# Gated factors of w_down loaded from ScalarE's queue, a new order of the seven products, and last weights split a step later

## The chip, the cores and the metric

The kernel runs on one core of a Trainium2 chip. The metric is the device time of one execution in microseconds, as the median of several runs. The names of the engines are those of the profile: PE (TensorE, the matmuls), DVE (VectorE), ACT (ScalarE), POOL (GpSimd) and SP (SyncE, which only starts transfers). Before the change the transfers spoken of here are started by SP and by POOL; the profile lists them as SPq and POOLq.

## The reference, cut to what matters

A block of an encoder works on 512 tokens of width 2048: RMSNorm, an input projection, an mLSTM with 4 heads beside a differential attention with 8, an output projection with residual, and then the channel mixer, in which the change lies. All inputs are float32.

```python
D_MODEL = 2048; D_FF = 5632
h2 = rmsnorm(x, norm2_g[l])
x = x + (jax.nn.silu(h2 @ w_gate[l]) * (h2 @ w_up[l])) @ w_down[l]
return rmsnorm(x, final_g)
```

## The kernel before, in words

**Numbers in two parts.** Matmuls take a rounded 32-bit type. So each factor is split: ACT writes the rounded part (`hi`, the cast of L98) and DVE the remainder (`lo`, L99), and three matmuls hi*hi, hi*lo and lo*hi make one product in PSUM. A split needs ACT, then DVE, for every tile that PE is to read.

**The down stage.** 16 of the 22 blocks of 256 rows of `w_down` go through a fast scheme that multiplies 2x2 blocks with seven products, P1 to P7, in place of eight. The 16 blocks make 4 chunks (`NSP`), and each chunk is done for two halves of the columns: 8 steps, which the text numbers `u` = 0 to 7, with chunk `ci = u // 2` and half `dg = u % 2`. A step goes through the seven names in the order of the list `DOWN`. Each product is 24 matmuls of 128x512, in two halves `h` of the contraction, 12 matmuls for each. In the first chunk ACT copies the products to the tiles `M` (L1088), afterwards DVE adds to them there (L1090).

**Its weights.** `left_factors` is a generator that yields one split weight factor for each half of a product; `factor` keeps it two factors, so one product, ahead of PE (`LAP`), and the tiles `whi` and `wlo` are rings of three. Per step it needs, for each half, the blocks B11, B22 and B21 as they are, and T1 and T3, sums of two blocks each: a plain load by SP (L889) with a second, accumulating load by POOL behind it (L891). These 512 KB loads fill the rings `raw` (first halves) and `raw2` (second halves), seven tiles each. P1 uses B11, P3 uses B22, P2 uses B21, P5 uses T1 and P7 uses T3. P6 uses B22 + T1, which DVE writes over B22 (L913), and P4 adds B21 to that (L915), again over B22. `upto` sets how far ahead loads are put into the program.

**Its gated factors.** The gate and up stage stores silu(gate)*up in DRAM, as the seven combinations that the scheme needs (`actv`). `variant` brings back the two 128x512 halves of one of them, 256 KB each (L956), and splits them to `A` tiles; they are what PE holds against the weight factors. The tile is `ra`, a ring of two, or `raw` for the first four names, which `group` asks for during its last call. Three more names come during step 0. Those of a next chunk come during the odd steps, one name per product. SP starts all of these loads.

**What sets the order of the work.** The code is written in one stream, and a scheduler places the instructions of each engine by priority, so the order on an engine is not always that of the code. An engine runs its own instructions in order: a DMA issue that waits for a buffer holds what stands behind it on that engine. In the built program, transfers started by SP and by ACT take turns on eight completion counters; a start waits until the transfer before it on its counter has landed.

**The tail.** After the down stage, `combine` adds the M tiles up, `proj_tok` does four more blocks of `w_down`, and the last two blocks and the final norm end the kernel. `last_weights` loads the weights of these last two blocks (L1171) and splits them, a piece at each call from `at`.

Of the kernel before, what the change touches and what calls it, by code (L numbers as in the profile page):

```python
# [19 lines left out]
NSP = 4  # L20
# [10 lines left out]
def build(nc, tc, ctx, a, out):  # L31
# [49 lines left out]
    V, SC, G, PE = nc.vector, nc.scalar, nc.gpsimd, nc.tensor  # L81
# [7 lines left out]
    c = {}  # L89
# [6 lines left out]
    def split(hi, lo, src, scale=None):  # L96
        if scale is None:
            SC.copy(hi, src)  # L98
            V.tensor_tensor(lo, src, hi.bitcast(F32), ALU.subtract)  # L99
        else:  # L100
            SC.activation(hi, src, AF.Copy, scale=scale)
            V.scalar_tensor_tensor(lo, src, scale, hi.bitcast(F32), ALU.mult, ALU.subtract)
# [734 lines left out]
    actv = dram.tile([4 * NSP, 7, 128, 256], F32, name="actv")  # L837
# [4 lines left out]
    def tW(tag, dt=F32, bufs=3):  # L842
        return pW.tile([128, 1024], dt, tag=tag, name=nm(tag), bufs=bufs)

    DOWN = ["P1", "P3", "P6", "P5", "P7", "P4", "P2"]
    more = []

    def tR():
# [2 lines left out]
    def left_factors():  # L851
        def loads(w, g):
            r = []
            for q in range(4):
                t = tW("raw", bufs=7)
                nc.sync.dma_start(t, a[w][g, q])
                r.append(t)
            return r

        def parts(src):  # L860
            hi, lo = tW("whi", F32R), tW("wlo", F32R)
            split(hi, lo, src)
            return hi, lo

        todo = [(w, g) for g in range(NFB) for w in ("w_g", "w_u")]
        nxt = loads(*todo[0])
        for i in range(len(todo)):
            w11, w12, w21, w22 = nxt
            yield parts(w11)
            s1 = tW("raw", bufs=7)  # L870
            V.tensor_tensor(s1, w21, w22, ALU.add)
            V.tensor_tensor(w21, w11, w21, ALU.subtract)
            V.tensor_tensor(w11, s1, w11, ALU.subtract)
            yield parts(w11)
            yield parts(w21)
            yield parts(s1)
            if i + 1 < len(todo):
                nxt = loads(*todo[i + 1])
            yield parts(w12)
            yield parts(w22)  # L880
            V.tensor_tensor(w12, w12, w11, ALU.subtract)
            yield parts(w12)


        def load(u, h, i, ring):
            j, n, j2, n2 = ((0, 0, 0, 0), (1, 1, 1, 1), (0, 0, 0, 1), (1, 1, 0, 1), (1, 0, 1, 0))[i]
            ci, dg = divmod(u, 2)
            t = ring()
            nc.sync.dma_start(t, a["w_ds"][ci, dg, j, n, h])  # L889
            if (j, n) != (j2, n2):  # L890
                G.dma_start(t, a["w_ds"][ci, dg, j2, n2, h], accum_op=ALU.add)  # L891
            return t

        order = [(u, i, h) for u in range(2 * NSP) for i in range(5) for h in range(2)]
        got = {}
        pos = [0]

        def upto(k):
            while pos[0] < min(k, len(order)):
                u, i, h = order[pos[0]]  # L900
                got[u, i, h] = load(u, h, i, tR if h and (u, i) != (0, 0) else lambda: tW("raw", bufs=7))
                pos[0] += 1

        upto(2)
        for u in range(2 * NSP):
            k = 10 * u
            for pi, name in enumerate(DOWN):
                if u or pi:
                    upto(k + (14 if pi == 0 else 16 if pi < 6 else 20))
                for h in range(2):  # L910
                    B11, B22, T1, T3, B21 = (got.get((u, i, h)) for i in range(5))
                    if name == "P6":
                        V.tensor_tensor(B22, B22, T1, ALU.add)  # L913
                    if name == "P4":
                        V.tensor_tensor(B22, B22, B21, ALU.add)  # L915
                    yield parts({"P1": B11, "P3": B22, "P6": B22, "P5": T1, "P7": T3, "P4": B22, "P2": B21}[name])
# [26 lines left out]

    cur_v = {}

    def variant(ci, name, into):

        v = ["P1", "P7", "P2", "P4", "P5", "P6", "P3"].index(name)
        into[name] = []
        for h in range(2):  # L950
            if more:
                r = more[2].tile([128, 512], F32, tag="ra", name=nm("ra"), bufs=2)
            else:
                r = tW("raw", bufs=7)[:, 0:512]
            g0 = 4 * ci + 2 * h
            nc.sync.dma_start(r.rearrange("p (g c) -> p g c", g=2), actv[g0:g0 + 2, v].rearrange("g p c -> p g c"))  # L956
            hi, lo = tA(), tA()
            split(hi, lo, r)
            into[name].append((hi, lo))

    def group(scale, done, first=False, last=False):

        banks = {}
        ps, u, C1, C2 = (tX() for _ in range(4))
# [45 lines left out]
        for name in order:  # L1010
            w = factor()
            product(bank(name), w, name_of(name))
            if first and name == "P2":
                next(st2)
            after(name)
            if last:
                i = {"P1": 0, "P6": 1, "P5": 2, "P4": 3}.get(name)
                if i is not None:
                    variant(0, DOWN[i], cur_v)

    def name_of(p):
        return RIGHT[p]
# [46 lines left out]
    for u in range(2 * NSP):  # L1069
        ci, dg = divmod(u, 2)  # L1070
        got_v = cur_v
        if dg == 1:
            cur_v = {}
        for pi, name in enumerate(DOWN):
            if u == 0 and pi < 3:
                variant(0, DOWN[4 + pi], cur_v)
            if dg == 1 and ci + 1 < NSP:
                variant(ci + 1, name, cur_v)
            banks = [tacc(), taux()]
            for h in range(2):  # L1080
                product_down(banks, factor(), name, h)
            if ci == 0:
                M[dg][name] = pM.tile([128, 1024], F32, tag="M", name=nm("M"), bufs=14)
            t = M[dg][name]
            for tt in range(2):
                cs = slice(tt * 512, tt * 512 + 512)
                if ci == 0:
                    SC.copy(t[:, cs], banks[tt])  # L1088
                else:
                    V.tensor_tensor(t[:, cs], banks[tt], t[:, cs], ALU.add)  # L1090
# [75 lines left out]
    def last_weights():  # L1166

        for b in range(CHUNKS[-1]):
            for n in range(4):
                r = tW("raw", bufs=7)  # L1170
                nc.sync.dma_start(r, a["w_d"][NFB - CHUNKS[-1] + b, n])  # L1171
                for j in range(2):
                    hi, lo = tL(), tL()
                    split(hi, lo, r[:, j * 512:j * 512 + 512])
                    wL[n][0].append(hi)
                    wL[n][1].append(lo)
                yield

    for ci, nb in enumerate(CHUNKS[:-1]):
        q = chunks[ci]  # L1180
# [31 lines left out]
    for tt in range(4):  # L1212
# [14 lines left out]
        r = tsm(1, tag="rf")  # L1227
# [99 lines left out]
```

## Time and profile before

| | |
|---|---|
| median of 3 runs | 2180.97 us |
| lowest and highest run | 2178.7 and 2186.47 us |
| the profiled execution's own time | 2190.05 us |
| span of the profiled execution | 2188.3 us |
| granted clock of PE, mean over the span | 0.991 |
| PE, DVE, ACT, POOL busy | 98%, 72%, 45%, 6% of the span |
| the down stage | 1691.3 to 2044.4 us of the span |

The span runs from the first to the last instruction that the profiler saw; the execution's own time has 1.75 us more around it. A busy share is one over stages with different limits, so the rows further down cut the down stage into its steps. A granted clock of 1.00 is 2.4 GHz, and the lower level is 1.2 GHz.

### The profile page before, as it was taken

Reading aid. Unit: us, or ns where it says so; the run is one execution under the profiler, and the core shown is the slowest. Engines: PE = TensorE matmul, PEld = TensorE weight load, DVE = VectorE, ACT = ScalarE, POOL = GpSimd, SP = SyncE. Lnnn points to the kernel's source line nnn. Section 1 sums busy time; section 2 is a strip of 40 time slices with the busy share of each in tenths; the row PEclk is TensorE's granted clock in tenths of the full one; section 3 lists DMA queues with packets and bytes.
Section 4 is the critical chain, followed back from the end, with each engine's and each line's share of the span. In section 5 each row is a group of like instructions: output and inputs, shape, how many; then the busy total and the mean of one; then the engine's idle time right before and its main releaser. Section 6 shows DMA issues by size and latency. Waiting matters only on the chain.

```text
span 2188.3 us, 33437 instructions
## 1 busy us (share of the span) xinstructions
PE 2142.0 (98%) x13305; PEld 1938.2 (89%) x13305; DVE 1569.6 (72%) x2362; ACT 992.7 (45%) x1515; POOL 133.8 (6%) x189
## 2 busy tenths in 40 slices
PE   9999999999999999999999999999999799999998
PEld 7888889988888889999999999999999577778786
DVE  6267776366544468888888888888889467779745
ACT  6256675355434354344344443343444454444423
POOL 0011110000000000000000000000000000001100
PEclk9999999999999999999999999999999999999999
DMA  6232112332234424343443434433335986876732
GB/s 257 96 96 78 62 53 72 116 97 87 82 112 146 140 92 131 124 145 119 129 135 119 137 121 133 131 123 117 121 121 168 284 228 184 242 210 156 203 106 77
DMA packets 100749, 292.56 MB, mean 134 GB/s; under 512 B 10976, under 2 KB 27376, under 8 KB 100592
## 3 DMA queue, kind: packets, MB, share of 16 engines
q1 hardware_dynamic: 86832, 247.42, 34.5%
q0 software_dynamic: 13760, 43.00, 8.4%
q8 instruction: 104, 1.70, 0.3%
q14 instruction: 53, 0.43, 0.1%
HBM read 264.16 MB, written 26.22 MB: 133 GB/s over the span
## 4 chain that ended last, share of the span: by engine, by line
PE 85%; DMA 6%; DVE 6%; ACT 2%; issue 1%; ACTq 0%; POOL 0%; DVEq 0%; SPq 0%; POOLq 0%
PE acc L159 9%; PE acc L158 9%; PE acc L160 9%; PE acc L933 8%; PE acc L932 8%; PE acc L931 8%; PE aux L933 6%; PE aux L932 6%; PE aux L931 6%; DMA ra<-actv 4%; PE acc L189 4%; PE acc L190 4%; PE acc L191 4%; DVE wlo L99 2%; PE aux L160 1%
## 5 line engine op out<-in xcount | busy, mean ns | idle before, releaser
L98 ACT CAST whi<-raw 128x1024 fp32r<-128x1024 f32 (+2 forms) x573 | 593.6, 1037 | 807.4 <-PE acc L932 238.8
L99 DVE TENSOR_TENSOR wlo<-raw,whi 128x1024 fp32r<-128x1024 f32 (+2 forms) x573 | 690.5, 1206 | 305.8 <-ACT whi L98 295.0
L158 PE MATMUL acc<-whi,A 128*128 128x512 f32 (+1 forms) x1056 | 404.0, 384 | 21.4 <-ACT whi L98 18.2
L159 PE MATMUL acc<-wlo,A 128*128 128x512 f32 (+1 forms) x1056 | 403.7, 382 | 9.5 <-DVE wlo L99 9.5
L160 PE MATMUL acc<-whi,A 128*128 128x512 f32 (+1 forms) x1056 | 400.7, 379 | 0.0
L158 PEld LDWEIGHTS acc<-whi,A 128*128 128x128 f32 x1056 | 200.0, 190 | 59.4 <-ACT whi L98 22.5
L159 PEld LDWEIGHTS acc<-wlo,A 128*128 128x128 f32 x1056 | 200.3, 190 | 48.0 <-DVE wlo L99 15.0
L160 PEld LDWEIGHTS acc<-whi,A 128*128 128x128 f32 x1056 | 200.4, 190 | 34.0
L932 PE MATMUL acc<-A,whi 128*128 128x256 f32 x704 | 199.3, 283 | 0.5 <-DVE A L99 0.5
L931 PE MATMUL acc<-A,whi 128*128 128x256 f32 x704 | 199.4, 283 | 0.0
L931 PE MATMUL acc<-h,whi 128*128 128x256 f32 x704 | 199.4, 283 | 0.0
L933 PE MATMUL acc<-h,wlo 128*128 128x256 f32 x704 | 199.2, 283 | 0.0
L932 PE MATMUL acc<-h,whi 128*128 128x256 f32 x704 | 199.2, 283 | 0.0
L933 PE MATMUL acc<-A,wlo 128*128 128x256 f32 x704 | 199.2, 283 | 0.0
L933 PE MATMUL aux<-h,wlo 128*128 128x256 f32 x528 | 149.7, 284 | 0.8 <-DVE wlo L99 0.8
L931 PE MATMUL aux<-h,whi 128*128 128x256 f32 x528 | 149.6, 283 | 0.6 <-ACT whi L98 0.6
L189 PE MATMUL acc<-A,whi 128*128 128x512 f32 x384 | 150.1, 391 | 0.0
L190 PE MATMUL acc<-A,whi 128*128 128x512 f32 x384 | 149.8, 390 | 0.0
L191 PE MATMUL acc<-A,wlo 128*128 128x512 f32 x384 | 149.8, 390 | 0.0
L933 PE MATMUL aux<-A,wlo 128*128 128x256 f32 x528 | 149.4, 283 | 0.0
L931 PE MATMUL aux<-A,whi 128*128 128x256 f32 x528 | 149.4, 283 | 0.0
L932 PE MATMUL aux<-A,whi 128*128 128x256 f32 x528 | 149.4, 283 | 0.0
(280 smaller groups left out, 4123.9 us busy)
## 6 DMA issues: line engine op xcount, KB each, us to landing
raw<-in_w_g_dram SPq DMA_DIRECT2D x88, 512.0 KB, 3.5
raw<-in_w_u_dram SPq DMA_DIRECT2D x88, 512.0 KB, 3.6
raw<-in_w_ds_dram SPq DMA_DIRECT2D x80, 512.0 KB, 5.1
raw<-in_w_aqk_dram SPq DMA_DIRECT2D x32, 512.0 KB, 3.4
raw<-in_w_o_dram SPq DMA_DIRECT2D x32, 512.0 KB, 3.5
raw<-in_w_ds_dram POOLq DMA_DIRECT2D x32, 512.0 KB, 8.2
raw<-in_w_b_dram SPq DMA_DIRECT2D x31, 512.0 KB, 4.0
actv<-x POOLq DMA_DIRECT2D x48, 256.0 KB, 3.4
```

The costliest lines, as they stand in the source:

```text
L98: SC.copy(hi, src)
L99: V.tensor_tensor(lo, src, hi.bitcast(F32), ALU.subtract)
L158: PE.matmul(acc, lh, rh, start=first, stop=False)
L159: PE.matmul(acc, lh, rl, start=False, stop=False)
L160: PE.matmul(acc, ll, rh, start=False, stop=last)
L189: PE.matmul(banks[f], wh[:, cs], xh[k], start=first, stop=False)
L190: PE.matmul(banks[f], wh[:, cs], xl[k], start=False, stop=False)
L191: PE.matmul(banks[f], wl[:, cs], xh[k], start=False, stop=last)
L931: PE.matmul(bank, w[0][:, cs], hi, start=m == 0, stop=False)
L932: PE.matmul(bank, w[0][:, cs], lo, start=False, stop=False)
L933: PE.matmul(bank, w[1][:, cs], hi, start=False, stop=m == 7)
```

## The change

It has three parts. (1) `DOWN` is now P1, P3, P2, P6, P5, P7, P4, and the loads of a step are put in the order B11, B22, B21, T1, T3. (2) `variant` is cut in two: `load_v` starts the two loads, now from ACT's queue (`SC.dma_start`), a product ahead of the split that `variant` still does. (3) In `last_weights` the `yield` stands between the load and its split.

```diff
--- before.py
+++ after.py
@@ -842,7 +842,7 @@
     def tW(tag, dt=F32, bufs=3):
         return pW.tile([128, 1024], dt, tag=tag, name=nm(tag), bufs=bufs)
 
-    DOWN = ["P1", "P3", "P6", "P5", "P7", "P4", "P2"]
+    DOWN = ["P1", "P3", "P2", "P6", "P5", "P7", "P4"]
     more = []
 
     def tR():
@@ -883,7 +883,7 @@
 
 
         def load(u, h, i, ring):
-            j, n, j2, n2 = ((0, 0, 0, 0), (1, 1, 1, 1), (0, 0, 0, 1), (1, 1, 0, 1), (1, 0, 1, 0))[i]
+            j, n, j2, n2 = ((0, 0, 0, 0), (1, 1, 1, 1), (1, 0, 1, 0), (0, 0, 0, 1), (1, 1, 0, 1))[i]
             ci, dg = divmod(u, 2)
             t = ring()
             nc.sync.dma_start(t, a["w_ds"][ci, dg, j, n, h])
@@ -906,9 +906,9 @@
             k = 10 * u
             for pi, name in enumerate(DOWN):
                 if u or pi:
-                    upto(k + (14 if pi == 0 else 16 if pi < 6 else 20))
+                    upto(k + (14 if pi == 0 else 16))
                 for h in range(2):
-                    B11, B22, T1, T3, B21 = (got.get((u, i, h)) for i in range(5))
+                    B11, B22, B21, T1, T3 = (got.get((u, i, h)) for i in range(5))
                     if name == "P6":
                         V.tensor_tensor(B22, B22, T1, ALU.add)
                     if name == "P4":
@@ -943,20 +943,26 @@
 
     cur_v = {}
 
-    def variant(ci, name, into):
-
+    loaded = []
+
+    def load_v(ci, name):
         v = ["P1", "P7", "P2", "P4", "P5", "P6", "P3"].index(name)
-        into[name] = []
         for h in range(2):
             if more:
                 r = more[2].tile([128, 512], F32, tag="ra", name=nm("ra"), bufs=2)
             else:
                 r = tW("raw", bufs=7)[:, 0:512]
             g0 = 4 * ci + 2 * h
-            nc.sync.dma_start(r.rearrange("p (g c) -> p g c", g=2), actv[g0:g0 + 2, v].rearrange("g p c -> p g c"))
+            SC.dma_start(r.rearrange("p (g c) -> p g c", g=2), actv[g0:g0 + 2, v].rearrange("g p c -> p g c"))
+            loaded.append((name, r))
+
+    def variant(into):
+
+        for h in range(2):
+            name, r = loaded.pop(0)
             hi, lo = tA(), tA()
             split(hi, lo, r)
-            into[name].append((hi, lo))
+            into.setdefault(name, []).append((hi, lo))
 
     def group(scale, done, first=False, last=False):
 
@@ -1016,7 +1022,9 @@
             if last:
                 i = {"P1": 0, "P6": 1, "P5": 2, "P4": 3}.get(name)
                 if i is not None:
-                    variant(0, DOWN[i], cur_v)
+                    if i:
+                        variant(cur_v)
+                    load_v(0, DOWN[i])
 
     def name_of(p):
         return RIGHT[p]
@@ -1072,10 +1080,16 @@
         if dg == 1:
             cur_v = {}
         for pi, name in enumerate(DOWN):
-            if u == 0 and pi < 3:
-                variant(0, DOWN[4 + pi], cur_v)
+            if u == 0 and pi < 4:
+                variant(cur_v)
+                if pi < 3:
+                    load_v(0, DOWN[4 + pi])
+            if ci + 1 < NSP and (dg, pi) == (0, 6):
+                load_v(ci + 1, DOWN[0])
             if dg == 1 and ci + 1 < NSP:
-                variant(ci + 1, name, cur_v)
+                variant(cur_v)
+                if pi < 6:
+                    load_v(ci + 1, DOWN[pi + 1])
             banks = [tacc(), taux()]
             for h in range(2):
                 product_down(banks, factor(), name, h)
@@ -1169,12 +1183,12 @@
             for n in range(4):
                 r = tW("raw", bufs=7)
                 nc.sync.dma_start(r, a["w_d"][NFB - CHUNKS[-1] + b, n])
+                yield
                 for j in range(2):
                     hi, lo = tL(), tL()
                     split(hi, lo, r[:, j * 512:j * 512 + 512])
                     wL[n][0].append(hi)
                     wL[n][1].append(lo)
-                yield
 
     for ci, nb in enumerate(CHUNKS[:-1]):
         q = chunks[ci]
```

Three places show how instructions move. `whi`, `A` and `M` are the tiles named above, the number behind a name is that of the tile, and `in_w_ds` is `w_down`.

SP at the start of step 0, before: 2812 and 2813 are the two halves of B22, 2814 and 2815 of T1, 2816 and 2817 of T3, 2818 of B21; 2820 and 2822 are blocks of step 1.

```order
L889 DMA raw_2812_17740<-in_w_ds_dram 128x1024
L889 DMA raw_2814_17744<-in_w_ds_dram 128x1024
L889 DMA raw_2816_17750<-in_w_ds_dram 128x1024
L889 DMA raw_2818_17756<-in_w_ds_dram 128x1024
L889 DMA raw_2820_17760<-in_w_ds_dram 128x1024
L889 DMA raw_2822_17764<-in_w_ds_dram 128x1024
L889 DMA raw2_2813_17742<-in_w_ds_dram 128x1024
L889 DMA raw2_2815_17747<-in_w_ds_dram 128x1024
```

And now, where 2808 and 2809 are B22, 2810 and 2811 B21, 2812 and 2813 T1, 2814 T3:

```order
L889 DMA raw_2808_17732<-in_w_ds_dram 128x1024
L889 DMA raw_2810_17736<-in_w_ds_dram 128x1024
L889 DMA raw_2812_17740<-in_w_ds_dram 128x1024
L889 DMA raw_2814_17746<-in_w_ds_dram 128x1024
L889 DMA raw2_2809_17734<-in_w_ds_dram 128x1024
L889 DMA raw2_2811_17738<-in_w_ds_dram 128x1024
L889 DMA raw2_2813_17743<-in_w_ds_dram 128x1024
```

The loads for step 1 have gone behind, B21 has come forward, and T1's second half stands seventh where it stood eighth. All loads of L956 have left SP in this stage.

ACT in step 0, before, from the casts for P3 (2812 and 2813 for the first time) over those for P6 (for the second) to those for P5 (2814, 2815):

```order
L98 CAST whi_2826_17774<-raw_2812_17740 128x1024
L98 CAST whi_2828_17790<-raw2_2813_17742 128x1024
L1088 COPY M_2830_17806<-acc_2810_17738 128x512
L1088 COPY M_2830_17806<-aux_2811_17739 128x512
L98 CAST whi_2839_17824<-raw_2812_17740 128x1024
L1088 COPY M_2843_17857<-acc_2837_17821 128x512
L98 CAST whi_2841_17841<-raw2_2813_17742 128x1024
L1088 COPY M_2843_17857<-aux_2838_17822 128x512
L98 CAST whi_2852_17874<-raw_2814_17744 128x1024
L98 CAST whi_2854_17890<-raw2_2815_17747 128x1024
```

And now, from the casts for P2 (2810, 2811) to the first for P6 (2808, for the second time):

```order
L98 CAST whi_2835_17813<-raw_2810_17736 128x1024
L1102 COPY M_2826_17796<-acc_2806_17730 128x512
L1102 COPY M_2826_17796<-aux_2807_17731 128x512
L956 DMA ra_2845_17858<-actv_7212 128x2x256
L98 CAST A_2853_17899<-ra_2844_17856 128x512
L98 CAST whi_2837_17829<-raw2_2811_17738 128x1024
L956 DMA ra_2878_18020<-actv_7212 128x2x256
L1102 COPY M_2839_17845<-acc_2833_17811 128x512
L1102 COPY M_2839_17845<-aux_2834_17812 128x512
L98 CAST whi_2848_17863<-raw_2808_17732 128x1024
L98 CAST A_2855_17903<-ra_2845_17858 128x512
L98 CAST A_2895_18081<-ra_2878_18020 128x512
```

P6's casts have come behind those of P2, and starts of factor loads stand between casts and copies.

ACT late in step 3, before, where the casts of factors (`A`) and weights (`whi`) alternate:

```order
L98 CAST whi_3122_19018<-raw2_3031_18648 128x1024
L98 CAST A_3125_19038<-ra_3124_19036 128x512
L98 CAST whi_3136_19058<-raw_3038_18686 128x1024
L98 CAST A_3128_19044<-ra_3127_19042 128x512
L98 CAST whi_3138_19074<-raw2_3039_18688 128x1024
L98 CAST A_3193_19374<-ra_3192_19372 128x512
L98 CAST whi_3144_19100<-raw_3040_18690 128x1024
L98 CAST A_3196_19380<-ra_3195_19378 128x512
L98 CAST whi_3146_19116<-raw2_3041_18692 128x1024
```

And now:

```order
L98 CAST whi_3106_18944<-raw_3038_18684 128x1024
L98 CAST A_3100_18934<-ra_3091_18892 128x512
L98 CAST whi_3108_18960<-raw2_3039_18687 128x1024
L956 DMA ra_3102_18938<-actv_7212 128x2x256
L956 DMA ra_3103_18940<-actv_7212 128x2x256
L98 CAST whi_3118_18993<-raw_2987_18409 128x1024
L98 CAST A_3110_18978<-ra_3102_18938 128x512
L98 CAST A_3112_18982<-ra_3103_18940 128x512
L98 CAST whi_3120_19010<-raw2_2988_18411 128x1024
L956 DMA ra_3114_18986<-actv_7212 128x2x256
```

Each product has two starts of L956 in this row, and one weight cast stands between a start and the cast of what it loads.

## Rows read from the trace of the kernel before

**Rows 1.** The page: busy us, share of the span and instructions of each engine.

```profile
PE 2142.0 (98%) x13305; PEld 1938.2 (89%) x13305; DVE 1569.6 (72%) x2362; ACT 992.7 (45%) x1515; POOL 133.8 (6%) x189
```

**Rows 2.** Busy time by stretch, steps 0, 1, 2, 3, 5, then the tail.

```profile
core 0: us, PE busy (x) PEld busy (x) DVE busy (x) ACT busy (x) POOL busy (x), PEclk, DMA share, GB/s
1691.30:1749.30 58.00, 44.98 (x184) 35.12 (x183) 28.62 (x30) 23.57 (x33) 8.04 (x10) 0.91 0.99 298
1749.30:1795.40 46.10, 42.15 (x169) 33.24 (x169) 29.37 (x32) 28.37 (x41) 3.41 (x4) 0.93 0.80 221
1795.40:1833.70 38.30, 38.30 (x170) 31.71 (x170) 29.93 (x33) 16.26 (x17) 3.40 (x4) 1.00 0.76 213
1833.70:1881.40 47.70, 42.01 (x168) 33.17 (x168) 37.01 (x45) 21.14 (x27) 3.40 (x4) 0.93 0.75 214
...
1919.70:1967.00 47.30, 42.18 (x169) 33.13 (x169) 37.16 (x46) 21.05 (x26) 3.42 (x4) 0.93 0.76 211
...
2044.40:2076.00 31.60, 29.00 (x122) 23.55 (x121) 18.79 (x23) 12.78 (x19) 6.93 (x8) 0.95 0.84 228
```

**Rows 3.** Waits, 1691.3 to 2044.4: engine, line, releaser: total us, times, longest.

```profile
ACT A L98 <- DMA ra<-actv: 69.4, 31, 6.2
...
ACT whi L98 <- DVE raw L913: 16.6, 5, 7.1
```

**Rows 4.** Chain of waits, step 0: start us, us, what.

```profile
1691.27 8.47 DMA raw<-in_w_ds_dram
...
1699.82 19.27 DMA ra<-actv
...
1720.49 8.99 DMA ra<-actv
```

**Rows 5.** Chain of waits, step 3.

```profile
1838.38 8.56 DMA ra<-actv
...
1861.21 9.65 DMA ra<-actv
```

**Rows 6.** Tile ra: its load, cast and remainder (ns min/median/max), and landing.

```profile
L956 SPq DMA_DIRECT2D ra<-actv x48: 359/377/378, 895.4 to 1960.1; - x48
L98 ACT CAST A<-ra x48: 611/621/628, 1687.8 to 1963.7; 128x512 fp32r<-128x512 f32 x48
L99 DVE TENSOR_TENSOR A<-ra,A x48: 680/686/694, 1688.9 to 1964.4; 128x512 fp32r<-128x512 f32 x48
...
DMA to landing us min/median/max: 2.6/4.3/19.3
```

**Rows 7.** ACT in order of time, step 0; in brackets idle before, and releaser.

```profile
1713.73 1.04 ACT L98 CAST whi<-raw 128x1024 fp32r<-128x1024 f32 x1 [7.12 <-DVE raw L913]
...
1729.50 0.62 ACT L98 CAST A<-ra 128x512 fp32r<-128x512 f32 x1 [5.29 <-DMA ra<-actv]
```

**Rows 8.** PE in order of time, step 0.

```profile
1703.88 0.50 PE L159 MATMUL acc<-wlo,A 128*128 128x512 f32 x1 [2.06 <-DVE wlo L99]
...
1714.83 0.80 PE L158 MATMUL acc<-whi,A 128*128 128x512 f32 x1 [5.45 <-ACT whi L98]
```

**Rows 9.** POOL in order of time, step 0.

```profile
1691.99 0.89 POOL L891 DMA_DIRECT2D raw<-in_w_ds_dram  x1 [36.82 <-DMA raw<-in_w_ds_dram]
```

**Rows 10.** DMA issues, 1690 to 1745: count, KB each, median us to landing.

```profile
raw<-in_w_ds_dram SPq DMA_DIRECT2D x17, 512.0 KB, 9.7
raw<-in_w_ds_dram POOLq DMA_DIRECT2D x8, 512.0 KB, 8.8
```

**Rows 11.** The page, costliest groups: count, busy us, mean ns of one.

```profile
L99 DVE TENSOR_TENSOR wlo<-raw,whi 128x1024 fp32r<-128x1024 f32 (+2 forms) x573 | 690.5, 1206 | 305.8 <-ACT whi L98 295.0
```

**Rows 12.** ACT in order of time, end of the gate and up stage.

```profile
1684.42 0.62 ACT L98 CAST A<-raw 128x512 fp32r<-128x512 f32 x1 [1.58 <-DMA raw<-actv]
```

**Rows 13.** Chain of waits, tail.

```profile
2052.68 7.46 DMA raw<-in_w_d_dram
...
2062.13 6.63 DMA raw<-in_w_d_dram
```

## The prediction

> **What bounds the kernel now.** The page comes first: PE is busy 2142.0 of 2188.3 us [rows 1], so all that can be won by better feeding is the idle 46 us, plus what slowed clocks cost. The next view is busy time by stretch, cut at the starts of the down stage's steps [rows 2]. Step 2 shows the stage undisturbed: 38.30 us for seven products, PE busy throughout, granted clock 1.00, so **5.47 us a product**. Step 0 takes 58.00, step 1 46.10, step 3 47.70 and step 5 47.30. Above 38.30 that is 19.7, 7.8, 9.4 and 9.0, together **45.9 us**. PE's own idle time is 13.0, 3.95, 5.7 and 5.1 of them; the rest is longer matmuls, since the granted clock there is 0.91 to 0.93, which is some stretches at 1.2 GHz between others at 2.4. The reader should see that the loss sits in step 0 and in the odd steps, those that fetch the next chunk's gated factors.
>
> The table of waits says what ended last there [rows 3]: ScalarE waited 69.4 us in 31 waits for the factors' loads, and 16.6 us in 5 for the sum of L913. The chain confirms it. In step 0 it runs through a weight load of 8.47 us and then one factor load that took **19.27** us to land, then one of 8.99 [rows 4]; in step 3 through factor loads of 8.56 and 9.65 [rows 5]. Tile ra's own median from issue to landing is 4.3 and its least 2.6 [rows 6], so the long ones stood behind SP's weight loads of 512 KB. ScalarE's order shows two waits of step 0: 7.12 us for the sum of L913 and 5.29 for a factor [rows 7]. PE's shows what comes of the first: idle 2.06 and then 5.45 us [rows 8].
>
> **The change, part by part.** The sum is made against the profiled execution (2190.05 us) and carried over to the median of the runs (2180.97), which is 9.1 lower.
>
> *Loads from ScalarE's queue.* The ra ring still has two buffers, and a load still waits for the remainder of the content before it. So a product's two loads start no earlier than before; what changes is the queue, and that ScalarE issues them. In an odd step ScalarE then has a loop per product: issue 0.38 (the issue on SP [rows 6]; POOL's 0.89 is the upper end [rows 9]), landing, two casts of 0.62 [rows 6], and one weight cast of 1.04 [rows 7] that now stands between issue and cast, as the order of step 3 shows. The remainder of 0.69 [rows 6] runs on DVE under the weight cast. The second issue overlaps the first landing.
>
> What a landing costs on its own queue no row shows. From below it is the least, 2.6 [rows 6]; from above 8.8, the accumulating loads, which have POOL's queue to themselves while SP's weight loads take 9.7 [rows 10]. A factor is 262 KB, so alone at the 298 GB/s of step 0 [rows 2] it moves in 0.88 us, and 1.7 of the 2.6 is fixed. Sharing the engines evenly with one queue gives 1.7 + 1.8 = 3.5, with two 4.3: my estimate is **4.0**, as SP's queue is always filled and POOL's at times. The size is that of ra, not of the 512 KB loads, so I stay near the low end.
>
> The loop is then 0.38 + 4.0 + 1.24 + 1.04 = 6.66 against 5.47 of PE, 1.2 too long, over the six products that follow the first: 7.2 us. The rings give back what they hold: factors are made one product ahead, 5.47 less a cast of 1.04 and its remainder of 1.21 [rows 11], so 3.2. What is left over is **L = 4.0 us per step**. Gains: step 1 7.8 - 4.0 = 3.8; step 3 9.4 - 4.0 = 5.4; step 5 9.0 - 4.0 = 5.0.
>
> SP loses two waiting issues per product and holds nothing but weight loads in the stage; no weight load ended a wait in steps 1 to 5, so this is worth nothing further.
>
> *The order of products.* P2 now stands third and P6 fourth, so the sum of L913 is needed 5.47 us later in step 0, and of the 7.12 us [rows 7] 1.65 stay. In SP's row T1's second half was the eighth of the weight loads and is now the seventh, so it lands no later. Step 0 has its own four factor casts, for which I take the same L: left over 4.0 + 1.65 = 5.65, a gain of 19.7 - 5.65 = **14.0**. In later steps the ring gives T1 the buffer that B22 or B21 leaves, and these are held until P4, the last product of the step before. From that cast, half a product into P7, to the cast for P6 are about four products, 21.5 us; a plain load and its accumulating load behind it take 9.7 + 0.9 + 8.8 = 19.4 even at step 0's pace [rows 9, 10]. Cost nothing, cover 2 us.
>
> *End of the gate and up stage.* Eight loads of factors move to ScalarE, 8 x 0.38 = 3.0 us, and its casts there wait 1.58 for such a load already [rows 12] without a gap on PE. Each of the four products has the 3.2 us of the rings. I take a loss of 1 (0 to 7.1, eight times POOL's 0.89). Two early ra loads are put at nothing: by twice 4.3 [rows 6] less twice 3.2 they cost 2.2 at most.
>
> *Last weights.* SP's six loads keep their order; only the splits come a step later. The tail has 31.60 - 29.00 = 2.6 us idle and a clock of 0.95 [rows 2], and its chain runs through landings of 7.46 and 6.63 [rows 13], so it could gain or lose about 4. Nothing issues earlier: taken as 0, with -4 and +4 kept for the range.
>
> Sum: 14.0 + 3.8 + 5.4 + 5.0 - 1 = 27.2. So 2190.05 becomes 2163, and the median 2180.97 becomes **2154**. As a formula, the change is -(43.25 - 4L).
>
> **A rule beside a row.** The long landings [rows 4, 5] against the least of 2.6 show that a factor waits out what is queued ahead of it. The Trainium skill, "DMA: Bandwidth & Descriptors", section "Queues, rings and completion order", says that an engine takes turns, a packet at a time, between the queues with work: by that the factor no longer waits out SP's backlog, and the landing is the shared 3.5 to 4.3. The same page, section "Issuing engines are not separate DMA queues", says that transfers run on the same 16 engines whichever engine starts them, and that starting them from several saves only issue time; that is the third case below. The trace of before has no load of ra from another queue, so neither is shown here.
>
> **The cases.**
>
> (a) The forecast, **0.50**: landing 3.5 to 4.3. At 3.5 the loop is 6.16, L = 1.0, change -39: 2142. At 4.3 L = 5.8, change -20: 2161. For it: the gap between 2.6 and the 19.27 behind the backlog.
>
> (b) Landing near the least, **0.15**: at 2.6 the loop is 5.26, under 5.47, L = 0, change -43: **2138**. For it: in the steps after 0 the DMA engines are busy 0.75 to 0.80 [rows 2], so a quarter is free. Against it: ScalarE's issue may cost more, and DVE's 37.01 us of work in step 3 [rows 2] nearly fill 38.3, so DVE becomes the bound there with nothing to spare.
>
> (c) The factors land no sooner, **0.20**: the DMA engines are 0.99 busy in step 0 [rows 2] whoever issues, and the odd steps' loop is bound by two buffers as before. Then only the order of products helps: the 2.06 and 5.45 idle [rows 8] with the slow clock's part beside them, 6.7 x 7.5/13.0 = 3.9, less the 1 above: -10.4, **2171**. For it: the 8.8 of POOL's own queue [rows 10].
>
> (d) Slower, **0.15**: ScalarE is held by its own issues. Before, SP did the waiting for a free buffer, or for a load that landed late, and ScalarE waited only for data. Now a DMA issue that waits stands in ScalarE's stream with weight casts behind it; since a load's completion counter is shared in turn with SP's loads, the issue can wait for a 512 KB load to land (9.7 in step 0 [rows 10]). This breaks even where 4L = 43.25, L = 10.8, a loop of 7.8, a landing with its waits of 5.1 us. At 6 us L is 16, change +21: **2202**. For it: the longest wait of ScalarE for ra was already 6.2 [rows 3]. Against it: ScalarE is busy only 21.14 of 47.70 us in step 3 [rows 2].
>
> That the change does nothing is part of (c): last weights alone would be such a part.
>
> **How the numbers follow.** About 0.3%, 6.5 us, is what a measurement here can tell from no change. (a) and (b) are faster; of (c), close to that bound, 0.11 is faster and 0.09 the same; of (d) 0.01 is the same and 0.14 slower. So faster 0.76, same 0.10, slower 0.14. The likeliest case's own range is 2142 to 2161. For 8 in 10 it must hold (b), with 2 us of the tail below it, and (c), and the mild part of (d) with landings up to 5.35: 2136 to 2186. What is left out is most of (d) and the far end of (b).
>
> **What would show it.** Right: ra's issues on ScalarE's queue with a median landing of 3.5 to 4.3 and none near 19; ScalarE's waits for ra under 40 us; step 0 near 44, steps 1, 3 and 5 near 42 us with clocks above 0.95; no wait of 7 us for the sum of L913; even steps still 38.3. Wrong: landings above 5, ScalarE idle ahead of its own issues, and PE waiting on whi in the odd steps (d); landings as before (c); a wait for T1's accumulated load in steps 1 to 7, by which the order costs what it gave; or PE gaps at the end of the gate and up stage.

## The result: slower, by 1.1%

| | before | the change |
|---|---|---|
| median of 4 runs each, us | 2183.3 | 2208.05 |
| lowest and highest, us | 2178.7 to 2186.47 | 2204.49 to 2209.51 |
| ratio to before, with its 95% interval | | 1.0113 (1.0088 to 1.0137) |
| span and granted clock of the profiled execution | 2188.3 us, 0.991 | 2207.7 us, 0.986 |

Some 25 us were lost where 27 were forecast as a gain (the 2180.97 of the forecast was the median of the first three of these four runs of before). The time lies above the range.

**The profile after.** First the page: busy us, share and instructions of each engine, and the DMA queues with packets, MB and share of 16 engines' span.

```profile
PE 2144.6 (97%) x13305; PEld 1941.7 (88%) x13305; DVE 1568.5 (71%) x2362; ACT 993.3 (45%) x1515; POOL 133.8 (6%) x189
...
q1 hardware_dynamic: 71600, 232.74, 32.1%
...
q10 hardware_dynamic: 15232, 14.68, 2.2%
```

PE's work is as before [rows 1], so the loss is waiting. A queue is new: q10 is ScalarE's, and it holds the factor loads alone. Its 14.68 MB went in 15232 packets, 0.96 KB each; SP's queue q1 has 3.25 KB a packet.

Next, busy time by stretch, with the columns of before: steps 0, 1, 3, 5 and 6 of the down stage [rows 2].

```profile
1693.00:1748.60 55.60, 43.66 (x171) 34.48 (x170) 27.59 (x29) 23.94 (x32) 7.97 (x10) 0.88 0.92 273
1748.60:1802.40 53.80, 41.63 (x172) 33.62 (x172) 29.68 (x31) 28.30 (x41) 3.40 (x4) 0.87 0.78 224
...
1839.90:1890.80 50.90, 43.34 (x170) 34.22 (x169) 36.77 (x45) 21.17 (x26) 3.40 (x4) 0.90 0.76 215
...
1929.00:1981.10 52.10, 43.35 (x173) 34.36 (x172) 36.91 (x45) 21.22 (x27) 3.43 (x4) 0.90 0.75 215
1981.10:2027.10 46.00, 40.83 (x169) 33.06 (x168) 36.62 (x40) 18.13 (x20) 6.85 (x8) 0.93 0.62 153
```

Against the same steps of before [rows 2]: step 0 took 55.60 and not 58.00, step 1 53.80 and not 46.10, step 3 50.90 for 47.70, step 5 52.10 for 47.30. The even steps 2 and 4 stayed (37.50 and 38.20). Step 6, which lost nothing to speak of before (39.80 us from 1967.00 to 2006.80), took 46.00. The stage also began 1.7 us later (1693.0 for 1691.3), as was put at 1, and the tail gave about 2 back (142.0 us from the stage's end to the span's end, where it had been 143.9). In all, -2.4 + 7.7 + 3.2 + 4.8 + 6.2 in these steps; the small rest of the stage adds 0.1. That makes the 19.4 us between the two spans; the medians lie further apart, 24.8, as the profiled execution of before was one of its slower ones.

The waits of the stage, 1693.0 to 2065.7: engine, line, releaser, total us, times, longest.

```profile
ACT A L98 <- DMA ra<-actv: 83.0, 22, 11.6
...
PE acc L158 <- ACT whi L98: 39.1, 8, 11.7
```

ScalarE waited 83.0 us for ra where it had waited 69.4 [rows 3], in fewer waits, but the longest is 11.6 and no longer 6.2. The wait for the sum of L913 has gone from ScalarE's list, as the new order promised. What it was worth was more than lost: PE waited 39.1 us for ScalarE's weight casts. The same wait before:

```profile
PE acc L158 <- ACT whi L98: 18.2, 7, 5.4
```

The chain of the stage, start us, us and what, has the long landings by place:

```profile
1693.04 15.67 DMA ra<-actv
1708.88 10.53 DMA ra<-actv
...
1775.52 16.45 DMA ra<-actv
...
1871.61 11.86 DMA ra<-actv
...
1961.60 12.13 DMA ra<-actv
...
2005.23 13.16 DMA raw<-actd
```

These are step 0 twice, then the longest of each of steps 1, 3 and 5, and in step 6 a load for the tail (`raw<-actd`, from SP's queue). Before, the long landings of step 3 were 8.56 and 9.65 [rows 5]. Now 11.9 to 16.5 us pass for 256 KB on a queue that holds nothing else. Step 1 at the place, ScalarE first, in order of time:

```profile
1775.52 0.37 ACTq L956 DMA_DIRECT2D ra<-actv  x1
1787.35 0.62 ACT L98 CAST A<-ra 128x512 fp32r<-128x512 f32 x1 [11.64 <-DMA ra<-actv]
...
1792.00 0.62 ACT L98 CAST A<-ra 128x512 fp32r<-128x512 f32 x1 [3.06 <-DMA ra<-actv]
1792.52 1.04 ACT L98 CAST whi<-raw 128x1024 fp32r<-128x1024 f32 x1
```

And PE:

```profile
1793.62 0.79 PE L158 MATMUL acc<-whi,A 128*128 128x512 f32 x1 [11.70 <-ACT whi L98]
```

The load starts at 1775.52. Between it and the next weight cast stand two factor casts that wait 11.64 and 3.06 us for landings. `A` is what the next step needs; `whi` is what PE needs now, and it stands behind. So PE loses 11.70 us. Tile ra's landing over the whole kernel (least, median, most) shows how little a median tells here:

```profile
DMA to landing us min/median/max: 2.5/3.9/16.5
```

The median is 3.9, just what was forecast. What decides is the long ones.

### The profile page after: what moved, and what is told of

Its sections match the earlier page's. It is cut to its first block, busy times and chain, and to the rows that moved or that the text cites. A ratio compares the mean times of both kernels' runs of the same rounds, so it can differ in the third digit from the quotient of the medians.

```text
span 2207.7 us, 33383 instructions
## 1 busy us (share of the span) xinstructions
PE 2144.6 (97%) x13305; PEld 1941.7 (88%) x13305; DVE 1568.5 (71%) x2362; ACT 993.3 (45%) x1515; POOL 133.8 (6%) x189
## 3 DMA queue, kind: packets, MB, share of 16 engines
q10 hardware_dynamic: 15232, 14.68, 2.2%
## 4 chain that ended last, share of the span: by engine, by line
PE 86%; DMA 6%; DVE 4%; ACT 2%; issue 1%; ACTq 0%; POOL 0%; DVEq 0%; POOLq 0%
PE acc L159 10%; PE acc L158 10%; PE acc L160 9%; PE acc L933 7%; PE acc L931 7%; PE acc L932 7%; PE aux L933 6%; PE aux L932 6%; PE aux L931 6%; DMA ra<-actv 4%; PE acc L190 4%; PE acc L189 4%; PE acc L191 4%; PE aux L160 2%; PE aux L158 2%; PE aux L159 2%
## 5 line engine op out<-in xcount | busy, mean ns | idle before, releaser
L158 PE MATMUL acc<-whi,A 128*128 128x512 f32 (+1 forms) x1056 | 405.4, 385 | 41.3 <-ACT whi L98 39.1
L158 PEld LDWEIGHTS acc<-whi,A 128*128 128x128 f32 x1056 | 200.8, 190 | 79.0 <-ACT whi L98 42.9
```

The source lines that it names most:

```text
L158: PE.matmul(acc, lh, rh, start=first, stop=False)
```

## Where the crowd comes from

The accumulating loads, which POOL starts, show a second difference. POOL in order of time around step 1, before:

```profile
1751.08 0.85 POOL L891 DMA_DIRECT2D raw<-in_w_ds_dram  x1 [20.78 <-DMA raw<-in_w_ds_dram]
1754.14 0.84 POOL L891 DMA_DIRECT2D raw<-in_w_ds_dram  x1 [2.21 <-DVE raw L913]
1771.02 0.85 POOL L891 DMA_DIRECT2D raw<-in_w_ds_dram  x1 [16.04 <-DVE wlo L99]
1774.60 0.86 POOL L891 DMA_DIRECT2D raw<-in_w_ds_dram  x1 [2.73 <-DVE wlo L99]
```

And with the change:

```profile
1772.52 0.84 POOL L891 DMA_DIRECT2D raw<-in_w_ds_dram  x1 [26.93 <-DVE A L99]
1774.78 0.84 POOL L891 DMA_DIRECT2D raw<-in_w_ds_dram  x1 [1.42 <-DMA raw<-in_w_ds_dram]
1776.51 0.85 POOL L891 DMA_DIRECT2D raw<-in_w_ds_dram  x1 [0.89 <-DMA raw<-in_w_ds_dram]
1778.31 0.86 POOL L891 DMA_DIRECT2D raw<-in_w_ds_dram  x1 [0.95 <-DMA raw<-in_w_ds_dram]
```

Before, they start in pairs, some 20 us apart. Now all four start within 6 us, at the moment when the odd step's factor load goes out (1775.52). The reason is in the order of the loads and the ring of seven, as the built program shows: T1 takes over the buffer of the step before that held B21. P4's sum reads that one, and P4 is now last. T3's buffer is free earlier, but its load stands behind T1's on SP. So all four plain loads go out together, and the accumulating ones behind them. Two theories followed. **O**: the new order alone gathers the loads. **Q**: ScalarE's queue is what slows the factors or ScalarE. A third was that it takes both.

## The experiments

Times are medians; every ratio is to runs of the kernel before on the same chip, with its 95% interval. Steps are measured from the last operation on `M` of one step to that of the next, so that kernels can be compared; by that measure the kernel before has 46.4, 47.8, 47.4 and 39.7 us for steps 1, 3, 5 and 6, and the change 53.8, 50.9, 52.1 and 46.0. Each is from one profiled execution. The kernel with the last weights alone has, in its built program, the same instructions in the same order as before on every engine up to the end of the down stage, and yet step 3 took 43.8 us in it and 47.8 before. So 4 us in one step can come and go without a cause in the program; of the change's steps, 1 and 6 stand clear of that and 5 barely; step 3, and the 2.4 us that step 0 gained, do not.

| run | median us | ratio | steps 1, 3, 5, 6 (us) |
|---|---|---|---|
| order alone | 2186.65 | 1.0015 (1.0004 to 1.0026) | 48.3, 45.6, 45.8, 45.5 |
| queue alone | 2187.24 | 1.0021 (1.0012 to 1.0030) | 45.4, 47.8, 47.1, 39.8 |
| last weights alone | 2182.62 | 0.9994 (0.9981 to 1.0008) | 47.3, 43.8, 46.8, 39.3 |
| change, rows of 2 KB | 2193.39 | 1.0045 (1.0030 to 1.0060) | 49.5, 47.6, 48.8, 45.5 |
| change, old load order from step 1 | 2191.96 | 1.0042 (1.0025 to 1.0059) | 49.0, 46.8, 46.4, 42.3 |
| change, three ra buffers | 2193.73 | 1.0052 (1.0036 to 1.0068) | 48.2, 49.2, 49.0, 45.8 |
| change, no accumulating loads | 2155.34 | 0.9874 (0.9858 to 0.9891) | 43.5, 39.3, 41.0, 38.0 |
| those three together | 2172.94 | 0.9957 (0.9942 to 0.9972) | 43.5, 43.0, 42.9, 42.6 |
| change, factor casts on POOL | 2203.61 | 1.0089 (1.0063 to 1.0115) | 49.7, 52.6, 53.0, 44.2 |
| three together, casts on POOL | 2175.24 | 0.9960 (0.9945 to 0.9974) | 43.8, 43.5, 42.7, 44.1 |
| old order, 2 KB rows, three buffers, ScalarE's queue | 2163.57 | 0.9907 (0.9878 to 0.9937) | 39.8, 40.9, 41.3, 38.6 |
| the same, SP's queue | 2165.59 | 0.9914 (0.9888 to 0.9939) | 41.2, 41.9, 43.1, 39.7 |

**The order alone**: `DOWN`, the order of the weight loads and `upto`; factors still come over SP.

```diff
-    DOWN = ["P1", "P3", "P6", "P5", "P7", "P4", "P2"]
+    DOWN = ["P1", "P3", "P2", "P6", "P5", "P7", "P4"]
-            j, n, j2, n2 = (..., (0, 0, 0, 1), (1, 1, 0, 1), (1, 0, 1, 0))[i]
+            j, n, j2, n2 = (..., (1, 0, 1, 0), (0, 0, 0, 1), (1, 1, 0, 1))[i]
```

> Only the new order of products and of weight loads; factors still loaded by SP. Theory O (the order gathers the weight loads that wait for P4 into a burst at the end of each odd step, and the factor loads are caught in it): slower than before by 12 to 25 us, one long landing of ra per odd step. Theory Q (ScalarE's queue is what costs): within 6 us of before, or faster by up to 10, since step 0's wait for the sum of L913 goes.

Slower, but by 0.15%, some 3 us: not O's 12 us, and within the 6 that Q allowed, though not a gain. The first and the last of POOL's four starts in step 1, and then two landings of the chain:

```profile
1766.54 0.84 POOL L891 DMA_DIRECT2D raw<-in_w_ds_dram  x1 [30.75 <-DMA raw<-in_w_ds_dram]
...
1780.89 0.86 POOL L891 DMA_DIRECT2D raw<-in_w_ds_dram  x1 [3.72 <-DVE A L99]
```

```profile
1771.81 10.05 DMA ra<-actv
...
1984.58 12.91 DMA raw<-actd
```

The four starts have gathered, but over 14 us. Factor loads wait in SP's row for their buffers and hold the weight loads behind them back. The landing in step 1 is 10.05 us. Step 6 is what costs: `raw<-actd` took 12.91 to land, and the step 45.5 us, nearly all that the changed kernel loses there. The shifts of 2 to 3 us in steps 0, 1, 3 and 5 are too small to be read from one execution.

**The queue alone**: `load_v` and `variant` as in the change, old order.

```diff
-            nc.sync.dma_start(r.rearrange("p (g c) -> p g c", g=2), ...)
+            SC.dma_start(r.rearrange("p (g c) -> p g c", g=2), ...)
```

> Only the factor loads moved to ScalarE's queue, a product ahead in the program; old order. Theory Q: slower than before by 12 to 25 us, long landings of ra on its own queue and ScalarE idle ahead of its casts. Theory O: faster by 5 to 25 us, landings of ra near 4 us in the odd steps. If only both parts together cost, e1 and e2 both lie within 8 us of before.

Slower by 0.2%, some 5 us: neither theory's number, and with the run before it the third case, in which only both parts together cost. The chain's landings:

```profile
1692.88 16.62 DMA ra<-actv
...
1774.27 10.14 DMA ra<-actv
...
1940.58 10.93 DMA ra<-actv
```

The first matters most: in step 0 the factor loads were alone on their queue, and one needed **16.62** us where behind SP's loads it had needed 19.27 [rows 4]. In steps 1 and 5 it took 10.14 and 10.93, much what SP's queue gave before; its chain there, and its landing of `raw<-actd` in step 6:

```profile
1772.53 9.61 DMA ra<-actv
...
1946.54 10.04 DMA ra<-actv
...
1992.62 5.38 DMA raw<-actd
```

A queue of its own gave the factors almost nothing.

**Last weights alone.**

```diff
+                yield
                 for j in range(2):
...
-                yield
```

> Only the last weights' split put a step later. Both theories: within 4 us of before, since SP's order stays as it is.

No difference, as expected.

**Rows of 2 KB.** The two groups of 256 tokens' halves that one load brings are stored side by side, so that a partition's row in DRAM is 2 KB and not twice 1 KB. Bytes and arithmetic stay.

```diff
-    actv = dram.tile([4 * NSP, 7, 128, 256], F32, name="actv")
+    actv = dram.tile([2 * NSP, 7, 128, 512], F32, name="actv")
-            SC.dma_start(r.rearrange("p (g c) -> p g c", g=2), actv[g0:g0 + 2, v].rearrange("g p c -> p g c"))
+            SC.dma_start(r, actv[g0 // 2, v])
```

> The changed kernel with the gated factors stored so that a row of a load is 2 KB and not 1 KB, the same bytes. If a queue's share of a busy stretch goes by the number of its pieces (in the changed kernel's profile ScalarE's queue has 0.96 KB a packet, SP's 3.25): the longest landings of ra fall from 12 to 16 us to 7 to 9, the gaps of PE in steps 1, 3 and 5 fall by half, and the time by 10 to 20 us, to 2188 to 2198. If it goes by bytes, or the loads wait for something else: within 5 us of the changed kernel, 2203 to 2213.

The ratio falls from 1.0113 to 1.0045, some 15 us by their difference, within the 10 to 20 expected from a share by pieces. ScalarE's queue on the page, and two landings of the chain:

```profile
q10 hardware_dynamic: 8064, 14.68, 2.1%
```

```profile
1770.80 12.88 DMA ra<-actv
...
1990.57 12.55 DMA raw<-actd
```

The same 14.68 MB now go in 8064 packets. The long landing of step 1 fell from 16.45 to 12.88, not to the 7 to 9 that a full halving would give; the longest on the chain in steps 3 and 5 are 9.29 and 10.26. SP's `raw<-actd` in step 6, whose rows did not change, still takes 12.55. So the number of pieces has a large part in it, and is not all. The Trainium skill, "DMA: Bandwidth & Descriptors", section "Queues, rings and completion order", has each engine taking turns between queues packet by packet; this run agrees in so far as the same bytes in half the packets landed sooner. How a single engine shares its time is not shown. The same page's section "Issuing engines are not separate DMA queues", by which loads run on the same 16 engines whichever engine starts them, agrees with the last two runs of the table (2163.57 and 2165.59).

**Old load order from step 1 on**, with the new order of products. T1 then takes a buffer that is free early in the step before, and only T3 waits for P4.

```diff
-        order = [(u, i, h) for u in range(2 * NSP) for i in range(5) for h in range(2)]
+        order = [(u, i, h) for u in range(2 * NSP) for i in ((0, 1, 3, 4, 2) if u else range(5)) for h in range(2)]
```

> The changed kernel, but from step 1 on the weight loads go in the old order (B11, B22, T1, T3, B21); the products keep the new one. Theory O+Q (T1 and T3 can be loaded only when P4, now last, lets go of B22 and B21, so their plain and accumulating loads come together late in the odd steps, while SP is no longer held back by the factor loads in its row; this gathering makes the long landings of ra): the accumulating loads of a step stand in pairs again, the longest landing of ra in the odd steps falls under 12 us, time 2180 to 2197. Rival R (ra on ScalarE's queue is slow beside any weight loads): within 5 us of the changed kernel, 2203 to 2213.

It came to 2191.96, inside the 2180 to 2197 of O and Q together, outside what R allowed. POOL around step 1:

```profile
1751.66 0.84 POOL L891 DMA_DIRECT2D raw<-in_w_ds_dram  x1 [16.29 <-DMA raw<-in_w_ds_dram]
1754.03 0.84 POOL L891 DMA_DIRECT2D raw<-in_w_ds_dram  x1 [1.53 <-DVE raw L913]
1773.59 0.85 POOL L891 DMA_DIRECT2D raw<-in_w_ds_dram  x1 [18.71 <-DVE A L99]
1777.64 0.86 POOL L891 DMA_DIRECT2D raw<-in_w_ds_dram  x1 [3.21 <-DMA raw<-in_w_ds_dram]
```

The pairs are back. The long landing there was 12.77, a little over the 12 expected. Of the 25 us about 15 went with the load order alone, plain and accumulating loads together.

**A third ra buffer**, with loads started three halves ahead.

```diff
-                r = more[2].tile([128, 512], F32, tag="ra", name=nm("ra"), bufs=2)
+                r = more[2].tile([128, 512], F32, tag="ra", name=nm("ra"), bufs=3)
...
+            if halves:
+                load_v(*halves.pop(0))
```

> The changed kernel with three ra buffers and the factor loads started half a product earlier still. Both theories: the landings stay long, 10 to 16 us, but half a product, 2.7 us, more of each is covered; three odd steps with two long landings each give 8 to 16 us, so 2192 to 2200. If ScalarE's wait for an issue's own turn were the cause, nothing is gained: 2203 to 2213.

As expected: 2193.73, and the longest landings of the odd steps stay at 13 us. That half a product more of each is covered is the expectation's account of the gain; the time fits it.

**No accumulating loads.** T1 and T3 keep only their first block; P5, P6 and P7 work with other weights, and 16 MB are not loaded.

```diff
-            if (j, n) != (j2, n2):
+            if False:
                 G.dma_start(t, a["w_ds"][ci, dg, j2, n2, h], accum_op=ALU.add)
```

> The changed kernel without the accumulating loads: T1 and T3 keep only their first block, so 16 MB less are loaded and P5, P6 and P7 use other weights. Theory O+Q: without POOL's four loads at a time the odd steps have no landing of ra over 9 us, and PE's gaps there vanish but for 1 to 3 us: 2155 to 2178. Rival: SP's own row of weight loads is enough to slow the factors: gaps of 4 us and more stay in steps 1, 3 and 5, 2185 to 2205.

At 2155.34 it is at the low end of O and Q. Tile ra's landing, least, median, most:

```profile
DMA to landing us min/median/max: 2.6/3.0/11.9
```

The 11.9 is step 0's; the odd steps have 7.20 at most on the chain, and steps 3, 5 and 6 come to 39.3, 41.0 and 38.0. ScalarE's queue, the factor's rows and the new order of products are all still there. Without POOL's transfers steps 3 and 5 stand only 1 to 3 us above the undisturbed 38.30, step 1 (43.5) some 5. So in the odd steps SP's row alone does not slow the factors by much, and POOL's loads are what they collide with. Whether it is by their bytes, by their gathering or by their being accumulated, this run does not tell, as it takes all three away. The run with the old load order says that the gathering has a part. The DMA queues in the change, from 1775 to 1792 us, when the load of 16.45 us was on its way (packets, MB, share of the 16 engines' time):

```profile
q0 software_dynamic: 576, 2.10, 63.3%
q1 hardware_dynamic: 418, 1.50, 24.2%
q10 hardware_dynamic: 806, 0.78, 14.2%
```

POOL's queue q0 holds only accumulating loads there. They took 63.3% of the engines' time for 2.10 MB, 30% for each MB, where SP's plain loads took 16%: an accumulated byte cost the engines nearly twice a plain one.

**All three mends together.** 

> The changed kernel with rows of 2 KB, three ra buffers and the old load order from step 1 on. If the gains of these add up where the theory puts them, the odd steps come to 39 to 42 us each and the time to 2155 to 2175, faster than both kernels; if each only moves the collision elsewhere, 2180 to 2195.

It came to 2172.94, faster than the kernel before by 0.4%, with odd steps of 43 us, just above the 39 to 42 expected. Step 6 (42.6) and step 0 lag.

**Factor casts on POOL.** This asks why PE pays for a factor that it needs only later.

```diff
-            split(hi, lo, r)
+            if more:
+                G.tensor_copy(hi, r)
+                V.tensor_tensor(lo, r, hi.bitcast(F32), ALU.subtract)
+            else:
+                split(hi, lo, r)
```

> The changed kernel with the cast of each factor that passes through ra, and the last name before them, made by POOL and no longer by ScalarE. Theory H (in the odd steps PE loses because the weight casts stand on ScalarE behind a cast that waits for ra; the factors themselves are needed only a step later): the landings stay long but PE's gap of 11.7 us in step 1 and of 5 in steps 3 and 5 fall to 0 to 3, time 2175 to 2195; a POOL cast costs perhaps 0.6 to 2 us and POOL has the time. Rival W (the weights themselves come late in the crowd of loads): the gaps stay, 2200 to 2215.

Not what H said: 2203.61, inside W's range. The waits, engine, line, releaser, total, times, longest:

```profile
POOL A L965 <- DMA ra<-actv: 83.8, 27, 9.3
ACT whi L98 <- DVE A L966: 78.6, 24, 10.1
DVE A L966 <- POOL A L965: 53.0, 22, 9.0
...
PE acc L159 <- DVE wlo L99: 39.4, 11, 8.1
...
PE acc L158 <- ACT whi L98: 2.4, 1, 2.4
```

POOL waits for ra in ScalarE's place. ScalarE still starts the loads, and a start waits for the remainder that frees the buffer: 78.6 us. But PE's wait for ScalarE's weight casts fell from 39.1 us to 2.4. In its place PE waits 39.4 us for the weights' remainders on DVE; these stand behind the factors' remainders (L966), and those wait 53.0 us for POOL's casts. So the line in which a weight stands behind a late factor has moved from ScalarE to DVE, and most of the loss with it. W has the time right but not the waits: from step 1 on ScalarE's weight casts waited 0.2 us in all for a weight load. A kernel in which neither cast, start nor remainder of a factor stands ahead of the weights was not tried, so that PE would then lose nothing is not shown.

> The version with 2 KB rows, three buffers and the old load order, with POOL's casts as well. Theory H: the gaps of 2 us left in the odd steps go, 2160 to 2172. Rival W: as without POOL's casts, 2170 to 2176, or slower where accumulating loads wait behind a cast on POOL.

Nothing either (2175.24 against 2172.94, intervals nearly the same), above the range that theory H gave and inside W's. PE's waits for the two parts of the weights come to 20.0 us in the stage and to 18.6 without POOL's casts.

**The old order with 2 KB rows and three buffers**, from ScalarE's queue and from SP's.

```diff
-            SC.dma_start(r, actv[g0 // 2, v])
+            nc.sync.dma_start(r, actv[g0 // 2, v])
```

> ScalarE's queue, 2 KB rows and three buffers, but products and loads in the order of before. If the new order of products still gives something once the landings are covered: slower than the version with the new products, 2175 to 2185. If it only costs: 2160 to 2170.

> As the last, but the loads of factors from SP's queue. If ScalarE's queue is worth something by itself: 5 to 15 us slower than the last. If the row size and the buffers do all: within 4 us of it.

2163.57 and 2165.59, **0.9% faster than the kernel before**, with intervals that overlap widely: with these rows and buffers it hardly matters which queue starts the loads. With the new order, its loads mended, the same rows and buffers gave 0.9957; the intervals stand apart. So the new order of products gave nothing here either, and was the slower by some 0.5%. The two kernels differ besides in the load order of step 0, in `upto`, and in the last weights, which alone made no difference. One wait in the down stage of the run on ScalarE's queue, and two landings of its chain:

```profile
ACT A L98 <- DMA ra<-actv: 28.2, 12, 4.8
```

```profile
1699.52 15.70 DMA raw<-in_w_ds_dram
...
1768.16 9.00 DMA ra<-actv
```

ScalarE's waits for ra have fallen from 69.4 [rows 3] to 28.2, though a landing of 9.00 is still there. A landing that is covered costs nothing. What stays is the 15.70 of a weight load in step 0. How much of the 0.9% comes from the rows, how much from the third buffer with its earlier starts, was not tried in the old order.

## Why the prediction was wrong

**The landing, the step on which the sum stood, was mis-sized.** It was put at 4.0 from the least landing and an even share of the bytes between queues. Overall the median came out at 3.9, but in step 0 it is 15.67 and 10.53, and in the odd steps 16.45, 11.86 and 12.13 where it mattered. So L, put at 4.0 us a step, came out at 15.5, 12.6 and 13.8 in steps 1, 3 and 5 (what they took above 38.30). The share was worked out by equal bytes, for which no row stood. The run with 2 KB rows shows that the size of the rows counts, and the queues at the long landing show that POOL's accumulating loads had 63.3% of the engines' time, not a share like the others'. The row of POOL's own queue, 8.8 us beside SP's 9.7 [rows 10], was the nearest evidence of what a queue gets in a crowd. It was kept as a bound when it was the better guide (though two stores of `actd` stood in that queue in the same stretch, so that it was not POOL's weight loads' alone). Case (c), that the factors land no sooner from another queue, had this right, and the queue alone bears it out.

**"Cost nothing, cover 2 us" for the order was wrong.** T1 was indeed in time for P6. But only T1's own deadline was asked for, not what its load, now in a bunch with three others, would do to loads beside it. That the bunch costs is shown by the old load order from step 1 on (15 us back). In step 0, where 14.0 us were forecast as a gain, 2.4 came, within what one execution differs from another: the wait for the sum of L913 went, the landings of 15.67 and 10.53 stayed.

**"SP holds nothing but weight loads, worth nothing further" was wrong too.** In the new order SP's waiting starts of factors spaced the weight loads: with them in SP's row the four accumulating starts spread over 14 us, without them over 6. This fits that each part alone cost 3 to 5 us and both together 25; a run that changes nothing but the spacing of these starts was not made.

**The slower rival (d) had the sign, the place and nearly the time** (2202 for 2208): ScalarE held, weight casts queued behind, PE waiting on `whi`. Its mechanism was off. No landing of an SP load held an issue in the rows of step 1; what held ScalarE there were the casts waiting for data. The landing it needed, over 5.1 us, was passed by far at a few places and not at most others (median 3.9), so that its time came so near is luck.

**What was right**: the end of the gate and up stage (1.7 us later, put at 1), last weights (nothing), the wait of ScalarE for the sum of L913 gone, the even steps 2 and 4 untouched. Step 6 was not in the sum at all; its 6.2 us come from the order, which puts SP's load for the tail into the same crowd (12.91 with the order alone, 5.38 before).

## What to carry to other kernels

Before moving a load to another queue, ask what its landing is made of: where the engines are busy, another queue changes little, while larger rows and one more buffer, with loads started earlier, took most of the same waits away here and made the kernel 0.9% faster. When an order of work changes, ask of every ring which buffers now come free at the same time, and what else is in flight then. A queue that waits is also a brake on what stands behind it; take the wait away and the brake goes too. And moving one instruction out of an engine's line helps only if no other engine then has the same line: with the factor casts on POOL, the weights waited on DVE instead.

## What the runs showed of the hardware that was not expected

A load of 256 KB with rows of 1 KB, alone on its queue, took 16.45 us to land beside 512 KB loads of two other queues, against 2.5 at its best; with rows of 2 KB and the same bytes it took 12.88 at the same place, and some 15 of the 25 us lost came back. In that crowd the accumulating loads took nearly twice the engines' time of plain ones for each MB: 63.3% for 2.10 MB, against 24.2% for 1.50. And two changes that cost 0.15% and 0.2% alone cost 1.1% together.
